# Score priority, a whole-bank norm and moved conditioning products in a two-layer decoder kernel

## The chip, the cores and the metric

The kernel runs on one core of one Trainium2 chip. The metric is the device time of one execution in microseconds (us); less is better. It is told as the median of several executions.

## What is computed

Two layers of a conditioned decoder trunk on a sequence of 256 tokens with 1024 features, all in float32. Each layer is three sublayers: a half-step SwiGLU FFN, a token mixer, and another half-step FFN. The mixer of the first layer is a gated linear recurrence (HGRN2), that of the second a causal gMLP. Every sublayer is wrapped in two RMS norms, and in a shift, a scale and a gate that come from a conditioning vector c.

```python
def sublayer(x, fn, pre_g, post_g, shift, scale, gate, res_w):
    h = rms_norm(x, pre_g) * (1.0 + scale) + shift
    return x + res_w * gate * rms_norm(fn(h), post_g)

mod = (silu(c) @ ada_w[i] + ada_b[i]).reshape(B, 9, D_MODEL)   # shift, scale, gate x 3

# recurrence, per chunk of 64 tokens and head (8 heads of 128)
o_inter = einsum('bhtk,bhkv->bhtv', qb * exp(bb), state)
decay   = exp(where(causal, bb[t] - bb[s], -inf))
scores  = einsum('bhtk,bhtsk,bhsk->bhts', qb, decay, kb)
o       = o_inter + einsum('bhts,bhsv->bhtv', scores, vb)
out     = (rms_norm(o, out_norm) * silu(g)) @ w_out            # norm per head
```

## The kernel before

**Sublayers and tiles.** The sublayers run one after the other: ffn0, the recurrence (called hg), ffn1, ffn2, the gMLP (gm), ffn3. Tokens lie in two tiles t of 128 rows; a tile of the result y is two halves h of 512 columns, each a bank of PSUM. Every matrix product is made of three matmuls on operands that are split into a high and a low part (L160 to L164 with 512 columns, L441 to L445 with 256, L400 to L420 for the first products of a sublayer, `pps`).

**Weights.** A weight block of 128x2048 comes in two halves. Each half is a 512 KB load `raw` on the SP queue (L57; four raw buffers, loads in program order), a cast to the high part on ACT (`cast`, L113 to L128), and a subtraction for the low part on DVE (`sub`, L129 to L135). `halves(n)` does n of both.

**Conditioning products.** The modulation is 144 products of 128x1024 on DVE (`ada`, L179 to L196; the product and the read-out of its sum are two rows at L192), each with a 512 KB load of its own on the SP queue and three buffers. `pace(upto, blocks, skip)` (L154) spreads them over the weight blocks of a sublayer, up to the cumulative target of the table `bgs` in `run`; the users `gate_tile` (L212, called through `G_fn`) and `pre_cols` (L197) force what is still missing when they are called.

**Boundary.** `boundary` (L297) leads from one sublayer to the next. Its instructions on ACT, DVE and PE stand in the hand-written order of the code: last products of y, squares of y (L233 to L236), mean and root, residual (L251), squares of x, the scaled row xn (L290), its transposes `npa` on PE (L264 to L277), the high part of h on ACT, and the full `hf` and the low part of h on DVE (L278 to L289). Everything else is ordered by the scheduler of the framework, by priority in program order.

**Recurrence.** `hgrn` (L627) first makes the projections `fps` and `tps` and the gates (`gate_f`, L666). `attn` (L693) then works one half of the heads (hb = 0, 1): for seven levels it scales q and k on DVE and ACT (tiles `t`), multiplies them on PE into scores (`ab`, L741, 64 columns; L701 and L761, 128 columns), merges each level's block by copy_predicated on DVE (L712), and at last multiplies the scores with v (L774, L776; called PV below). `finish` (L781) takes the norm per head (128-column squares on ACT, L787; a product from PSUM on DVE for each 128 columns, L800), transposes the result on PE (`ots`, L805) and splits it (L809, L810) for the output product y (`out_mm`, L395). `zip_steps` (L837) interleaves the generator of `attn` with fill work: projections of the second half, and for the second loop the products `outs` of the first half.

**gMLP.** `gmlp` (L912) makes the v half, calls `G_fn`, loads three columns of constants and then runs the u half in units.

## Time and profile before

| | |
|---|---|
| executions | 1199.64, 1200.78, 1204.22 us; median 1200.78 |
| the profiled execution | 1199.71 us, span 1197.9 us |
| PE busy | 1144.4 us, 96% of the span |
| DVE busy | 909.9 us, 76% |
| ACT busy | 663.3 us, 55% |
| bytes moved | 282.31 MB, 236 GB/s in the mean |
| granted clock of PE, mean | 0.982 |

The profile's lines name a line of the kernel, an engine, an operation and its tiles as out<-in. PE is TensorE, PEld its weight loads, DVE is VectorE, ACT is ScalarE, SP the queue that issues the loads. Behind a group stands the idle time of its engine just before it and what ended it. The waits view groups PE's idle time by the waiting line and by what it waited for: total, times, longest. A window's row gives each engine's busy time, then the granted clock of PE, the share of DMA and GB/s.

### The profile page before, as it was taken

The page shows a single profiled execution, that of the slowest core. Times are in us where ns is not written, and L with a number is a line of the kernel's source. Part 1 is how long each engine was busy: PE and PEld are TensorE (multiplying, and loading weights), DVE is VectorE, ACT ScalarE, POOL GpSimd, SP SyncE. Part 2 cuts the span into 40 slices and gives each one's busy share as a digit, 9 for nine tenths or more (in the row PEclk, how much of TensorE's full clock was granted, in tenths as well). Part 3 has the DMA queues.
Part 4 walks back from the last instruction along what each step waited for, and adds up shares of the span by engine and source line. Part 5 has one row for each costly group of instructions (what it writes and reads, how often), then busy time and mean ns, then how long its engine had stood idle before and what let it go on. Part 6 is the DMA issues. An engine that isn't in the chain of part 4 may idle for free.

```text
span 1197.9 us, 17119 instructions
## 1 busy us (share of the span) xinstructions
PE 1144.4 (96%) x6518; PEld 997.4 (83%) x6518; DVE 909.9 (76%) x1391; ACT 663.3 (55%) x1054; POOL 6.8 (1%) x16
## 2 busy tenths in 40 slices
PE   7999998898798899999999999999999999999997
PEld 6989997798787688888788888877798997888886
DVE  6987786779867789985589986476898777866642
ACT  6454446668547755555565555553664456645531
POOL 0000000000000000000000000000000000000000
PEclk9999999898899999999999999999999999999999
DMA  9889898296305389986279996426687764766630
GB/s 349 311 315 331 320 351 287 95 327 233 125 35 193 106 293 365 333 307 224 94 261 339 344 334 227 165 80 222 234 316 276 265 201 131 247 216 226 207 106 36
DMA packets 79764, 282.31 MB, mean 236 GB/s; under 512 B 9873, under 2 KB 10561, under 8 KB 79682
## 3 DMA queue, kind: packets, MB, share of 16 engines
q1 hardware_dynamic: 78626, 278.05, 66.0%
q0 software_dynamic: 1056, 3.17, 0.8%
q8 instruction: 51, 0.84, 0.3%
q14 instruction: 31, 0.25, 0.1%
HBM read 280.11 MB, written 1.07 MB: 235 GB/s over the span
## 4 chain that ended last, share of the span: by engine, by line
PE 83%; DVE 8%; DMA 4%; ACT 4%; issue 1%; SPq 0%; DVEq 0%; ACTq 0%
PE ups L437 17%; PE ups L438 9%; PE y L162 8%; PE y L163 8%; PE y L164 8%; PE pps L412 7%; PE ups L557 4%; PE ups L445 4%; PE ups L443 4%; PE ups L444 4%; DVE w L132 2%; PE ab L741 2%; DMA raw<-in_wffn 2%; ACT w L122 1%; PE vps L1003 1%
## 5 line engine op out<-in xcount | busy, mean ns | idle before, releaser
L132 DVE TENSOR_TENSOR w<-raw,w 128x1024 fp32r<-128x1024 f32 x376 | 453.8, 1223 | 113.5 <-ACT w L122 105.5
L122 ACT CAST w<-raw 128x1024 fp32r<-128x1024 f32 x376 | 387.1, 1050 | 167.7 <-DMA raw<-in_wffn 66.0
L437 PE MATMUL ups<-h,w 128*128 128x512 f32 x864 | 302.0, 393 | 0.0
L438 PE MATMUL ups<-h,w 128*128 128x256 f32 x864 | 242.0, 280 | 0.0
L437 PEld LDWEIGHTS ups<-h,w 128*128 128x128 f32 x864 | 161.7, 187 | 36.4
L192 DVE CUSTOM_DVE_ANT_0 ada<-ada,cond 128x1024 f32<-128x1024 f32 x144 | 173.6, 1221 | 21.7 <-DMA ada<-in_ada 21.7
L162 PE MATMUL y<-w,t 128*128 128x512 f32 x448 | 179.7, 402 | 0.0
L163 PE MATMUL y<-w,t 128*128 128x512 f32 x448 | 178.2, 398 | 0.3 <-DVE w L132 0.3
L164 PE MATMUL y<-w,t 128*128 128x512 f32 x448 | 177.7, 397 | 0.0
L438 PEld LDWEIGHTS ups<-h,w 128*128 128x128 f32 x864 | 163.3, 189 | 1.0
L445 PE MATMUL ups<-h,w 128*128 128x256 f32 x416 | 117.9, 283 | 2.1 <-DVE rs_sd L89 1.2
L443 PE MATMUL ups<-h,w 128*128 128x256 f32 x416 | 118.3, 284 | 0.0
L444 PE MATMUL ups<-h,w 128*128 128x256 f32 x416 | 117.7, 283 | 0.0
L412 PE MATMUL pps<-w,h 128*128 128x512 f32 x480 | 115.1, 396 | 0.2 <-DVE h L287 0.2
L412 PEld LDWEIGHTS pps<-w,h 128*128 128x128 f32 x480 | 89.9, 190 | 19.2 <-DVE h L287 0.6
L164 PEld LDWEIGHTS y<-w,t 128*128 128x128 f32 x448 | 84.6, 189 | 20.3
L162 PEld LDWEIGHTS y<-w,t 128*128 128x128 f32 x448 | 84.7, 189 | 18.9
L163 PEld LDWEIGHTS y<-w,t 128*128 128x128 f32 x448 | 84.7, 189 | 18.9 <-DVE w L132 1.4
L445 PEld LDWEIGHTS ups<-h,w 128*128 128x128 f32 x416 | 79.7, 191 | 2.5 <-DVE w L132 2.5
L443 PEld LDWEIGHTS ups<-h,w 128*128 128x128 f32 x416 | 79.7, 192 | 1.0 <-issue 0.2
L444 PEld LDWEIGHTS ups<-h,w 128*128 128x128 f32 x416 | 79.7, 192 | 0.8 <-issue 0.2
L80 ACT ACTIVATE t<-t 128x256 f32<-128x256 f32 (+2 forms) x70 | 36.6, 524 | 50.4 <-DVE t L490 41.7
(196 smaller groups left out, 1327.1 us busy)
## 6 DMA issues: line engine op xcount, KB each, us to landing
raw<-in_wffn SPq DMA_DIRECT2D x264, 512.0 KB, 5.5
ada<-in_ada SPq DMA_DIRECT2D x144, 512.0 KB, 6.7
raw<-in_wgmu SPq DMA_DIRECT2D x48, 512.0 KB, 5.0
raw<-in_whg SPq DMA_DIRECT2D x40, 512.0 KB, 5.2
raw<-in_wgmv SPq DMA_DIRECT2D x24, 512.0 KB, 5.0
G<-gflat POOLq DMA_DIRECT2D x6, 512.0 KB, 5.1
t<-in_gbin SPq DMA_DIRECT2D x6, 256.0 KB, 5.6
x<-in_x SPq DMA_DIRECT2D x2, 512.0 KB, 4.3
```

Of the source, the lines that this page charges most:

```text
L122: self.after(self.nc.scalar.copy(hi[:, sl], raw), self.hold[0])
L132: self.after(self.nc.vector.tensor_sub(lo[:, sl], raw, hi[:, sl]), self.hold[1])
L162: self.paced(mm(ps, l[0], r[0], start=start, stop=False))
L163: mm(ps, l[0], r[1], start=False, stop=False)
L164: mm(ps, l[1], r[0], start=False, stop=stop)
L192: self.after(nc.vector.tensor_tensor_reduce(t, t, self.cond, 1.0, 0.0, ALU.mult, ALU.add, self.mod[i // 24][:, i % 24:i % 24 + 1]), self.h ...
L412: lambda g=g, i=i, j=j, kc=kc, w=w: mm(res[g][t], h2[:, i, t, kc, :], w, start=kc + i + j == 0, stop=i == 1 and kc == KC - 1)))
L437: self.paced(mm(ps, u[0], self.h2[:, :, :, kc, :], start=kc == 0, stop=False))
L438: self.last = mm(ps[:, 1, :], u[1], self.h2[:, 0, :, kc, :], start=False, stop=kc == KC - 1)
L443: self.paced(mm(o, u[0], h[0], start=start, stop=False))
L444: mm(o, u[0], h[1], start=False, stop=False)
L445: self.last = mm(o, u[1], h[0], start=False, stop=stop)
```

## The change

- *Scores:* the steps of `attn` are wrapped in a raised scheduler priority (offset 400).
- *Norm:* `finish` is split into `stats`, `turn` and `split`. The squares are one ACT instruction for a whole bank into SBUF, with a sum on DVE; the gate product is one DVE instruction for a bank, and the scale by r is made on SBUF. For the second half of the heads all of this stands in a hand-written order, with 5 of the 16 output products ahead, 1 between the two groups of transposes, and the rest behind.
- *Boundary:* the mean of the squares of x is taken after both halves; the second half's `hf` is made on ACT; its low part comes behind the residual of the second tile; 35 instead of 30 products of the next sublayer stand ahead of the second transposes; how many casts stand where is a parameter.
- *Conditioning:* cumulative targets 40 after ffn0 (was 46) and 120 after ffn2 (was 118); in the recurrence they are spread over 14 blocks (was 9).
- *gMLP:* `G_fn` moves into the u loop (u = 8), and the three constants are loaded in ffn0.

```diff
@@ residual, h_low
-                if h == 0:
-                    self.half_mean(st)
+        if st is not None:
+            self.half_mean(st)
...
+    def h_full(self, h, pa, cols, scalar=False):
...
+            if scalar:
+                nc.scalar.activation(hf[:, ks], pa[:, ks], AF.Identity, bias=sh[:, kc:kc + 1], scale=A[:, kc:kc + 1])
+            else:
+                nc.vector.tensor_scalar(hf[:, ks], pa[:, ks], A[:, kc:kc + 1], sh[:, kc:kc + 1],
+                                        op0=ALU.mult, op1=ALU.add)
+        return hf
@@ boundary
+    def boundary(self, y, G, mm, cols, table, plan=(4, 2, 0, 0)):
...
-        self.halves(4)
+        self.halves(plan[0])
...
-        self.halves(2)
+        self.halves(plan[1])
...
+        for _ in range(plan[2]):
+            self.cast()
         self.residual(0, yg, r, sx)
+        for _ in range(plan[2]):
+            self.sub()
...
-        self.h_low(0, 0, pa0, cols)
-        self.h_low(0, 1, pa1, cols)
-        w = [[self.ready.pop(0) for _ in range(2)] for _ in range(2)]
-        self.res, go = self.proj(w)
+        self.h_low(0, 0, self.h_full(0, pa0, cols))
         sq(1, 1, sy1)
         gated(1, 1, yg1)
         r = self.inv_rms(sy1)
-        self.cast()
+        for _ in range(plan[3]):
+            self.cast()
+        hf = self.h_full(1, pa1, cols, scalar=True)
         self.residual(1, yg1, r, sx1)
-        self.sub()
+        for _ in range(plan[3]):
+            self.sub()
+        self.h_low(0, 1, hf)
+        w = [[self.ready.pop(0) for _ in range(2)] for _ in range(2)]
+        self.res, go = self.proj(w)
...
-        do(p0[0:30])
+        do(p0[0:35])
...
+        self.halves(1)
         self.table(table)
@@ hgrn
-        self.pace(bg, 9)
+        self.pace(bg, 14)
...
+        def attn(hb, bank, res):
+            gen = attn_steps(hb, bank, res)
+            while True:
+                with tc.high_priority(offset=400):
+                    if next(gen, gen) is gen:
+                        return
+                yield
...
+        def stats(hb, ops, sqrt):
...
+            for u in range(2):
+                sqs.append(self.t2().rearrange("p (i v) -> p i v", i=4))
+                nc.scalar.activation(sqs[u], ops[u].rearrange("p t h v -> p (t h) v"), AF.Square)
...
+                nc.vector.tensor_mul(og[:, 512 * u:512 * u + 512].rearrange("p (t c) -> p t c", t=NT),
+                                     ops[u].rearrange("p t h v -> p t (h v)"), gg[:, :, c0:c0 + 2 * P])
...
+                nc.vector.reduce_sum(ss[:, 4 * u:4 * u + 4], sqs[u], axis=mybir.AxisListType.X)
...
+        def turn(hb, u, og, r):
+            on = og[:, 512 * u:512 * u + 512].rearrange("p (i v) -> p i v", i=4)
+            for i in range(4):
+                nc.vector.tensor_scalar(on[:, i, :], on[:, i, :], r[:, 4 * u + i:4 * u + i + 1], None, op0=ALU.mult)
+            ps = self.acc.tile([P, 512], F32, tag="acc", name="ots")
...
-        finish(1, ops[1], True)
+        self.ahead = 0
+        fill = products(1)
...
+        self.open()
+        self.gate = state["ops"]
+        for op in fill[:5]:
+            op()
+        og, r = stats(1, ops[1], True)
+        ps = [turn(1, 0, og, r)]
+        fill[5]()
+        ps.append(turn(1, 1, og, r))
+        self.sub()
+        for op in fill[6:]:
+            op()
@@ gmlp
-        G = G_fn()
...
+            if u == 8:
+                G = G_fn()
@@ run
-        bgs = {"ffn0": 46, "hg": 64, "ffn1": 92, "ffn2": 118, "gm": 138, "ffn3": 144}
+        bgs = {"ffn0": 40, "hg": 64, "ffn1": 92, "ffn2": 120, "gm": 138, "ffn3": 144}
...
+                    self.boundary(y, G, mm, st["cols"], tables[subs[s + 1][0]], (2, 1, 1, 1) if s == 1 else (4, 2, 0, 0))
```

Lines behind L258 have other numbers in the changed kernel: scores are L758 (before L741), merges L729 (L712), `ots` L845 (L805), and the scale by r is L841.

On ACT at the end of ffn0, before; `t` is the last unit's activation there, `junka` takes the squares of y and of x:

```order
L80 ACTIVATE t_2008<-ups 128x512
L122 CAST w<-raw 128x1024 x3
L167 CAST t_2009<-t_2008 128x512
L74 ACT_TABLE_LOAD
L122 CAST w<-raw 128x1024 x9
L235 ACTIVATE junka,s_2091<-y_784 128x512
L122 CAST w<-raw 128x1024 x2
L235 ACTIVATE junka,s_2091<-y_785 128x512
```

The same place in the changed kernel:

```order
L80 ACTIVATE t_1996<-ups 128x512
L122 CAST w<-raw 128x1024 x4
L167 CAST t_1997<-t_1996 128x512
L74 ACT_TABLE_LOAD
L122 CAST w<-raw 128x1024 x6
L235 ACTIVATE junka,s_2079<-y_790 128x512
L122 CAST w<-raw 128x1024 x2
L235 ACTIVATE junka,s_2079<-y_791 128x512
```

Nine casts stood between the table load and the first square, and six stand there now; the other three come earlier.

On PE in the second score loop, before, where the first half's result is transposed (`ots`), with scores `ab` of two levels around it:

```order
L164 MATMUL tps<-w,h_2198 128x512
L741 MATMUL ab<-t_3441 128x64 x8
L805 MATMUL ots<-ident,t_3495 128x128 x4
L805 MATMUL ots<-ident,t_3509 128x128 x4
L741 MATMUL ab<-t_3521 128x64 x8
L162 MATMUL y_3536<-w 128x512
```

The same place in the changed kernel:

```order
L164 MATMUL tps<-w,h_2186 128x512
L845 MATMUL ots<-ident,t_3452 128x128 x5
L758 MATMUL ab<-t_3506 128x64 x8
L758 MATMUL ab<-t_3553 128x64 x8
L845 MATMUL ots<-ident,t_3452 128x128 x3
L162 MATMUL y_3521<-w 128x512
```

The transposes now stand ahead of the scores of two levels, and the level that came just ahead of them before (t_3441, now t_3435) is done earlier among the `tps` products.

On DVE in the second score loop, before, up to the first products with r (L800):

```order
L735 TENSOR_TENSOR t_3413<-t_3413,w 128x32x16
L788 TENSOR_SCALAR ss_3456<-ss_3456 128x8
L88 TENSOR_SCALAR rs_sh<-ss_3456 128x8
L91 TENSOR_SCALAR rs_hv<-ss_3456 128x8
L89 TENSOR_SCALAR rs_sd<-rs_sh 128x8
L98 TENSOR_TENSOR rs_q<-rs_sd 128x8
L735 TENSOR_TENSOR t_3441<-t_3441,w 128x64x8
L712 COPY_PREDICATED t_3290<-lmask,ab 128x16x32
```

The same loop in the changed kernel, between the merge of a level (L729) and the first sum of squares (L823):

```order
L729 COPY_PREDICATED t_3275<-lmask,ab 128x32x16
L132 TENSOR_TENSOR w<-raw,w 128x1024
L192 ISA ada,mod_108<-ada,cond 128x1024
L192 ISA mod_108 128x1
L192 ISA ada,mod_108<-ada,cond 128x1024
L192 ISA mod_108 128x1
L132 TENSOR_TENSOR w<-raw,w 128x1024 x2
L192 ISA ada,mod_108<-ada,cond 128x1024
L192 ISA mod_108 128x1
L823 TENSOR_REDUCE ss_3450<-t_3453 128x4
L819 TENSOR_TENSOR t_3452<-ab,w 128x512
```

Before, no conditioning product stood between the first scores of this loop and its `ots`; now eight stand there, with subs of weights between them.

More of the change, by code (lines that the diff above doesn't have):

```diff
@@ L295, in scaled, with open @@
             self.nc.scalar.activation(xn[:, hs], self.x[t][:, hs], AF.Copy, scale=r)
-    def boundary(self, y, G, mm, cols, table):
-        nc = self.nc
+    def open(self):
         E = mybir.EngineType
@@ L779, in attn @@
             yield
-        def finish(hb, ops, sqrt=False):
+        def attn(hb, bank, res):
[6 more added lines that the diff above has]
+        def stats(hb, ops, sqrt):
             ss = self.tiny.tile([P, 8], F32, tag="ss8", name="ss8")
-            o4 = [o.rearrange("p t h v -> p (t h) v") for o in ops]
+            r = self.tiny.tile([P, 8], F32, tag="r8", name="r8")
+            og, sqs = self.t4(), []
@@ L784, in finish, with gated @@
             for u in range(2):
-                for i in range(4):
-                    junk = self.scr.tile([P, 512], BF16, tag="junka", name="junka")
-                    nc.scalar.activation(junk[:, 0:P], o4[u][:, i, :], AF.Square, accum_out=ss[:, 4 * u + i:4 * u + i + 1])
+                sqs.append(self.t2().rearrange("p (i v) -> p i v", i=4))
+                nc.scalar.activation(sqs[u], ops[u].rearrange("p t h v -> p (t h) v"), AF.Square)
+            def gated(u):
+                c0 = 2 * (2 * hb + u) * P
+                nc.vector.tensor_mul(og[:, 512 * u:512 * u + 512].rearrange("p (t c) -> p t c", t=NT),
+                                     ops[u].rearrange("p t h v -> p t (h v)"), gg[:, :, c0:c0 + 2 * P])
@@ L788, in finish @@
+            for u in range(2):
+                nc.vector.reduce_sum(ss[:, 4 * u:4 * u + 4], sqs[u], axis=mybir.AxisListType.X)
+                if u == 0:
+                    gated(0)
             nc.vector.tensor_scalar(ss, ss, 1.0 / P, EPS, op0=ALU.mult, op1=ALU.add)
-            r = self.tiny.tile([P, 8], F32, tag="r8", name="r8")
             if sqrt:
                 self.tact(ss, ss, AF.Sqrt)
+                self.cast()
+                gated(1)
                 nc.vector.reciprocal(r, ss)
@@ L793, in finish @@
             else:
+                gated(1)
                 self.rsqrt(r, ss)
[L795 to L811 removed]
@@ new lines, in stats @@
+            return og, r
+        def turn(hb, u, og, r):
[3 more added lines that the diff above has]
+            ps = self.acc.tile([P, 512], F32, tag="acc", name="ots")
+            for i in range(4):
+                c0 = (i % 2) * S + (i // 2) * P
+                nc.tensor.transpose(ps[:, c0:c0 + P], on[:, i, :], self.ident)
+            return ps
@@ L813, in hgrn, with split @@
+        def split(hb, u, ps):
+            pair = 2 * hb + u
+            if not oall:
+                oall.extend([self.wtile() for _ in range(2)])
+            oT = [o[:, 512 * pair:512 * pair + 512] for o in oall]
+            nc.scalar.activation(oT[0], ps, AF.Copy, scale=self.onorm)
+            nc.vector.scalar_tensor_tensor(oT[1], ps, self.onorm, oT[0], op0=ALU.mult, op1=ALU.subtract)
+            oTs.append([o.rearrange("p (h s) -> p h s", h=2) for o in oT])
         ybank = {"i": 0}
@@ L907, in hgrn @@
         wos.append(nb())
+        self.open()
[8 more added lines that the diff above has]
+        for op in fill[6:]:
+            op()
+        for u in range(2):
+            split(1, u, ps[u])
         nxt(y, G, self.out_last(y, oTs[2:], wos))
@@ L1083, in late_consts @@
         self.onorm = self._load("onorm", [P, 1])
+        self.gm_cols = [self._load(n, [P, 24]) for n in ("gbinu", "glng", "glnb")]
     def first_h(self, kc):
@@ L1127, in nxt @@
                 else:
-                    self.boundary(y, G, mm, st["cols"], tables[subs[s + 1][0]])
+                    if s != 1:
+                        self.open()
+                    self.boundary(y, G, mm, st["cols"], tables[subs[s + 1][0]], (2, 1, 1, 1) if s == 1 else (4, 2, 0, 0))
                     self.hT = self.h2[:, 0], self.h2[:, 1]
```

67 lines of the change are left out of this document (24 added, 43 removed).

## Prediction

> **What bounds the kernel now.** I read the page first, then PE's waits, then the granted clock, then single stretches. The page says whose time it is:
>
> ```profile
> PE 1144.4 (96%) x6518; PEld 997.4 (83%) x6518; DVE 909.9 (76%) x1391; ACT 663.3 (55%) x1054; POOL 6.8 (1%) x16
> ```
>
> PE works for all but 53.5 of the span's 1197.9 us, and the change removes no matrix product. So it can pay only in idle time of PE and in time at a lowered clock. The waits of PE, grouped (total, times, longest), name the idle time that the edits aim at:
>
> ```profile
> PE npa L271 <- DVE be L242: 9.7, 2, 8.1
> PE npa L271 <- DVE xn L293: 7.5, 4, 2.4
> PE ab L741 <- DVE t L735: 6.6, 1, 6.6
> PE ab L741 <- ACT L L679: 5.1, 1, 5.1
> PE ots L805 <- DVE t L800: 5.0, 1, 5.0
> ```
>
> The windows cut where the granted clock changes show the second cost. After its name each row has the length, PE busy, PEld, DVE, ACT, POOL, clock, DMA share, GB/s:
>
> ```profile
> 208.79:219.03 10.24, 5.52 (x17) 4.63 (x18) 5.97 (x16) 5.95 (x16) 0.00 (x0) 0.50 0.40 142
> 287.29:297.53 10.24, 8.37 (x39) 8.40 (x40) 9.91 (x19) 7.63 (x20) 0.00 (x0) 0.50 0.72 252
> 311.19:321.43 10.24, 6.76 (x24) 6.12 (x25) 8.82 (x16) 5.22 (x7) 0.00 (x0) 0.50 0.28 100
> 382.87:386.28 3.41, 3.41 (x11) 2.37 (x11) 3.15 (x9) 1.91 (x3) 0.00 (x0) 0.50 0.46 156
> 410.17:413.59 3.42, 3.42 (x12) 2.72 (x11) 3.21 (x6) 2.25 (x7) 0.00 (x0) 0.50 0.63 165
> 840.25:843.67 3.42, 3.42 (x10) 2.66 (x9) 3.42 (x4) 1.67 (x4) 0.52 (x1) 0.50 0.71 242
> ```
>
> At clock 0.50, u us of busy PE do the work of u/2, so these stretches cost 2.8, 4.2, 3.4, 1.7, 1.7 and 1.7. Losses by place: **A**, ffn0 to recurrence, 8.1 + 2.8 = 10.9. **B**, the score stalls of the recurrence, 5.1 + 6.6 + 4.2 + 3.4 = 19.3. **C**, the last `ots` transposes, 5.0 + 1.7 = 6.7. **D**, recurrence to ffn1, (9.7 - 8.1) + 2.4 + 1.7 = 5.7. **E**, the three later boundaries, 7.5 - 2.4 = 5.1. **F**, start of the gMLP's u half, 3.7 (rows there).
>
> **The change part by part.** *A.* PE, then ACT, then the chain of waits:
>
> ```profile
> 213.51 1.11 PE L271 MATMUL npa<-ident,xn 128*128 128x128 f32 x4 [8.09 <-DVE be L242]
> ```
>
> ```profile
> 202.04 0.59 ACT L235 ACTIVATE junka<-y 128x512 bf16<-128x512 f32 x1
> 207.17 0.59 ACT L235 ACTIVATE junka<-y 128x512 bf16<-128x512 f32 x1
> ```
>
> ```profile
> 183.35 6.53 DMA raw<-in_wffn
> 192.42 5.84 DMA raw<-in_whg
> 200.63 5.57 DMA raw<-in_whg
> ```
>
> ```profile
> 160.00:180.00 20.00, 20.00 (x146) 18.91 (x146) 15.74 (x20) 7.89 (x11) 0.56 (x1) 1.00 0.98 345
> ```
>
> Row squares stand behind casts on ACT, casts behind weights that land late, in a stage whose DMA is full (0.98). Six fewer conditioning loads (46 to 40) take 6 x 512 KB, at 345 GB/s 9.1 us, out of that queue. In ACT's order three of nine casts move ahead of the table load before the first square. Taking the mean after both halves saves about 0.8 more. Needed: 8.1. I take a gap of 0.4 without half clock: gain 10.5. Least gain 3.3 (mean 0.8, two subs fewer at 1.22), if casts or the four raw buffers, not DMA, set the pace; most 10.9. Should the squares become early, the next late thing is the residual chain; ffn1 to ffn2 has the same chain and no first gap.
>
> *Recurrence, B.* Prices:
>
> ```profile
> L132 DVE TENSOR_TENSOR w<-raw,w 128x1024 fp32r<-128x1024 f32 x38 | 45.6, 1224 | 9.3 <-ACT w L122 9.2
> L192 DVE CUSTOM_DVE_ANT_0 ada<-ada,cond 128x1024 f32<-128x1024 f32 x18 | 21.5, 1223 | 0.8 <-DMA ada<-in_ada 0.8
> L712 DVE COPY_PREDICATED t<-lmask,ab 128x512 f32<-128x512 int32 x14 | 12.6, 899 | 13.1 <-PE ab L741 12.9
> L735 DVE TENSOR_TENSOR t<-t,w 128x512 f32<-128x512 f32 x14 | 9.7, 691 | 0.9 <-ACT t L80 0.9
> L800 DVE SCALAR_TENSOR_TENSOR t<-ab,r,w 128x128 f32<-128x128 f32 x16 | 4.4, 345 | 0.1
> ```
>
> ```profile
> 289.17 1.09 PE L741 MATMUL ab<-t 128*128 128x64 f32 x4 [5.09 <-ACT L L679]
> ```
>
> ```profile
> 202.17 1.23 DVE L132 TENSOR_TENSOR w<-raw,w 128x1024 fp32r<-128x1024 f32 x1 [0.21 <-ACT w L122]
> 203.31 0.15 DVE L242 TENSOR_SCALAR be<-s 128x1 f32<-128x1 f32 x1
> ```
>
> ```profile
> 204.79 0.40 PE L163 MATMUL y<-w,t 128*128 128x512 f32 x1
> 205.02 0.39 PE L164 MATMUL y<-w,t 128*128 128x512 f32 x1
> ```
>
> With priority the first score loop becomes one burst on DVE: 19 operations of 512 columns (0.691), 7 merges (0.899), 2 of half width (0.35 each by halving), one conditioning product and one sub (1.3, 1.2), 2 others (0.7). That is 24, less 0.09 of overlap for each of 32 (the sub at 202.17 lasts 1.23, its successor starts after 1.14): about 21. Begun near 288, where the stall that ends at 289.17 lies, it ends at 309, and PE does not wait 6.6 in between. B's 19.3 is thus won here.
>
> But the moved work falls on the second loop. Between the end of the first and the norm's first scale, DVE's new order has 8 subs (9.8), 10 conditioning products (13.1 with their read-out), 17 operations of 512 (11.7), 4 merges (3.6), 14 gate steps of 256 or 512 columns (8.0, by 0.3 to 0.7 each), 2 products of the output gate and 2 sums (2.8), 2 adds of the identity (1.4) and some 20 tiny ones (3.5): 54, less 85 x 0.09, so 46.4. DVE reaches the scale at 309 + 46.4 = 355.4. PE meanwhile has 73 products of 512 at 0.233 (204.79 to 205.02) = 17.0, 32 of 64 columns and 25 of 128 (4.3 and 7, by 0.14 to 0.28 each): 28 to 30, and waits about 2.8 for the scores of level 64 (half of the 5.1 at the first level before). So it is at the five `ots` transposes, which now stand ahead of the scores of levels 4 and 2, at 337 to 342; I take 341. PE stalls there 14.5 (13.5 to 18.5), 17.3 with level 64, then 3.4 of clock as after the 6.6 before: 20.7 lost. **B: 19.3 - 20.7 = -1.4.** DVE in the whole stage, before:
>
> ```profile
> 232.30:397.50 165.20, 146.54 (x954) 134.39 (x952) 133.41 (x225) 105.90 (x193) 1.08 (x2) 0.93 0.53 185
> 334.50:397.50 63.00, 56.16 (x334) 48.71 (x334) 48.49 (x91) 40.14 (x87) 0.69 (x2) 0.97 0.37 126
> ```
>
> Six products add 7.9 and the norm about 3 to its 133.4, some 144 of the stage's 165, while PE without losses needs 146.5 less the 9.3 of half clock, 137: DVE becomes the tighter engine there. At best, with its work spread, the stage loses nothing in the second loop: +19.3 for B.
>
> *C.* The norm was 8 squares and 8 products of 128 columns from PSUM (0.345) for a half; now two whole-bank squares (0.59, as the square at 202.04), two sums, two gate products and 8 scales. The sum has no row: between 0.15 (202.17's successor) and 0.899; I take 0.69, as an add of the same width. The scale of 128 columns from SBUF: 0.15 to 0.345; I take 0.25. Chain to the first four transposes: 2 x 0.59 + 2 x 0.69 + 0.69 + 0.15 + 0.3 + 0.15 + 4 x 0.25 = 4.9 with handovers 5.5; the 15 products put ahead cover 3.5. Gap 2.0 instead of 5.0. Gaps of 1.6 to 2.0 brought no half clock, one of 2.4 did (the stretch at 410.17), so I count part of 1.7: C gains 3.0 (0 to 6.7). The Trainium skill, "TensorE: Matmul & The Clock Gate", section "Why this matters for your kernels", puts the gap that halves the clock at over about 3 us; by it this term would be 3.7 and not 3.0, but the 2.4 us gap here shows that less is enough. The same skill, "VectorE: DVE Perf Modes", section "Rules for kernel authors", calls a reduce the slowest operation and advises against it on a hot path, which speaks against the two sums; at the merge's 0.9, the slowest row of that width, each adds 0.2, and the term would be 2.6. No run here shows a reduce of this form.
>
> *D.* One cast and two subs (1.05 + 1.22 + 1.22) now stand ahead of the second half's low part of h, which the 20th product of the next stage needs just in time elsewhere: a wait of about 3.5 and 1.7 of clock, for 5.7 before: +0.4 (-2 to +5.7). Recurrence in all: -1.4 + 3.0 + 0.4 = **2** (-5 to +24).
>
> *E.* PE waits at the boundary ffn1 to ffn2, and DVE there:
>
> ```profile
> 598.80 0.66 PE L271 MATMUL npa<-ident,xn 128*128 128x128 f32 x4 [1.57 <-DVE xn L293]
> ```
>
> ```profile
> 591.65 1.37 DVE L284 TENSOR_SCALAR hf<-npa,A,shift 128x128 f32<-128x128 f32 x4
> 593.06 0.69 DVE L287 TENSOR_TENSOR h<-hf,h 128x512 fp32r<-128x512 f32 x1
> 596.00 0.15 DVE L242 TENSOR_SCALAR be<-s 128x1 f32<-128x1 f32 x1 [0.79 <-ACT junka L235]
> ```
>
> The `hf` and sub from 591.65 leave the chain (2.0), the mean's wait at 596.00 goes (0.8): 2.85 earlier, and five more products ahead of the transposes (5 x 0.233 = 1.2) cover: no gap at three places. The sub now comes behind the residual, due about when it is needed: I charge 0.3. **4.8** (2.5 to 5.1).
>
> *F.* DVE, then PE:
>
> ```profile
> 834.61 1.23 DVE L192 CUSTOM_DVE_ANT_0 ada<-ada,cond 128x1024 f32<-128x1024 f32 x1 [4.81 <-DMA ada<-in_ada]
> ```
>
> ```profile
> 837.79 0.27 PE L219 MATMUL gps<-ident,gate 128*8 128x128 f32 x1 [1.15 <-DVE w L924]
> 838.93 0.50 PE L163 MATMUL pps<-w,h 128*128 128x512 f32 x1 [0.86 <-DVE w L132]
> ```
>
> The gate needs 120 products and only 118 were done; DVE stands 4.8 for the load of the last two with `w` behind it. Now 120 are done in ffn2, where two more (2.6 us of DVE) hide behind a PE that is never idle, and the gate is built later: 1.15 + 0.86 + 1.7 = **3.7** (1 to 4.5).
>
> *Three small loads* go into ffn0's start, where DMA is full: -0.5 (-1.5 to 0; most: the raw wait of one weight).
>
> **Sum.** 10.5 + 2 + 4.8 + 3.7 - 0.5 = 20.5. The profiled execution took 1199.71 us (1.1 under the median of 1200.78), so 1179.2, against the median 1180.
>
> **The rivals.** *1, the second loop does not stall:* DVE runs ahead of my count (13.1 us of idle before merges, in the L712 row, could take the products), `ots` finds its tile ready, the recurrence gains 2 + 17: 1163. For it: 165 - 144 = 21 us of slack in the stage. Against: the products stand in DVE's order behind the first burst. *2, casts or buffers set the pace at A:* gain 3.3 there instead of 10.5: 1187. For it: casts end each link of the chain in turn; against: full DMA. *3, slower:* in the second loop DVE waits for each conditioning load with three buffers, and everything up to `ots` waits behind it. The longest such wait in the trace is 6.4:
>
> ```profile
> DVE ada L192 <- DMA ada<-in_ada: 21.7, 9, 6.4
> ```
>
> Five such add 32 at `ots`: 1212. It decides once that stall passes 14.5 + 20.5 = 35, and is over the bound below at 41. Against: the DMA share there, 0.37. *4, little comes:* the recurrence at -2, A 3.3, E 2.5, F 1, the small loads -1: 3.8, so 1197.
>
> **How the numbers follow.** Mine 0.54, rival 1 0.22, rival 2 0.13, rival 3 0.05, rival 4 0.06. The range takes my case, rival 2 and part of rival 1: 1161 to 1193. A measurement here can tell 0.5%, 6 us, from no change: faster (under 1194.8) 0.88, same 0.07, slower 0.05.
>
> **What would show it.** PE's wait before the first transposes of h for the recurrence under 1 (A); no wait before scores in the first loop; a wait of some 14 before `ots` in the second loop, with half clock behind it (B; none is rival 1, over 35 rival 3); about 2 before the last `ots` (C); a wait of `pps` for the low part of h at recurrence to ffn1 (D); no wait of `npa` at the three later boundaries (E); none of DVE for a conditioning load in the gMLP (F). A time outside 1161 to 1193 would refute the sum; no stall at `ots` would refute B's count.

## The result, and the profile after

The changed kernel takes 1190.51 us in the median of four executions (1187.75 to 1192.97), the kernel before 1202.49 beside it. The ratio is 0.9911, 95% interval [0.9888, 0.9933]. The profiled executions stand 1187.75 against 1199.71: 12.0 us less, where the prediction's sum said 20.5. The time lies inside the range, and the gain is 59% of what the sum had.

The page, then PE's waits of the changed kernel (total, times, longest):

```profile
span 1186.0 us, 17085 instructions
...
PE 1138.3 (96%) x6518; PEld 992.1 (84%) x6518; DVE 906.2 (76%) x1379; ACT 665.9 (56%) x1046; POOL 6.8 (1%) x16
```

```profile
PE ots L845 <- DVE t L841: 18.1, 2, 15.6
PE vps L1059 <- DVE t L1066: 4.4, 4, 2.1
...
PE pps L429 <- DVE h L293: 3.1, 1, 3.1
...
PE tps L163 <- DVE w L132: 2.3, 1, 2.3
...
PE npa L271 <- DVE be L242: 2.2, 2, 1.9
...
PE fps L462 <- DVE w L132: 0.8, 1, 0.8
PE ab L718 <- DVE t L719: 0.7, 1, 0.7
```

The two waits of scores (6.6 and 5.1) are gone, and so is every wait of `npa` for xn (7.5). In their place stands one wait of 15.6 us at the first `ots`. The wait of `vps` in the gMLP is new; the prediction had nothing there.

The windows of the changed kernel at the lowered clock; the first row is the entry of the recurrence, the second stands behind the wait of `tps`, and the last two are the parts of one stretch before and after PE resumes at `ots`:

```profile
206.97:210.38 3.41, 3.41 (x12) 2.73 (x11) 1.71 (x6) 2.54 (x7) 0.00 (x0) 0.50 0.41 163
...
312.78:319.61 6.83, 5.71 (x13) 4.47 (x14) 6.81 (x10) 4.94 (x12) 0.55 (x1) 0.50 0.52 182
...
340.09:353.50 13.41, 0.00 (x0) 0.03 (x1) 13.24 (x38) 2.11 (x2) 0.00 (x0) 0.50 0.55 193
353.50:363.98 10.48, 10.48 (x45) 9.99 (x46) 6.38 (x13) 5.40 (x7) 0.00 (x0) 0.50 0.66 228
```

By u/2 they cost 1.7, 2.9 and 5.2. While PE stands still from 340.09 to 353.50, DVE is busy for 13.24 of 13.41 us: it is late, not idle.

The losses of PE by place, idle time and half clock, from the waits and the clock of both traces; gain is before less after:

| place | before | after | gain | forecast |
|---|---|---|---|---|
| start of ffn0 (idle) | 8.7 | 9.4 | -0.7 | -0.5 |
| A, entry of the recurrence | 8.1 + 2.8 | 1.9 + 1.7 | 7.3 | 10.5 |
| recurrence, with C and the exit's first wait | 18.7 + 9.3 | 22.5 + 8.1 | -2.7 | 1.6, and a part of D |
| exit, second part | 2.6 + 1.7 | 3.1 + 0 | 1.3 | rest of D's 0.4 |
| E, three later boundaries | 5.1 | 0 | 5.1 | 4.8 |
| F, gMLP | 4.1 + 1.7 | 4.4 + 0 | 1.4 | 3.7 |
| end | 6.3 | 6.4 | -0.1 | 0 |

Together 11.6 of the 12.0 us. Half clock at the start of ffn0 is left out of the first row: in both kernels the first products there take 0.42 us each instead of 0.28, for a stretch that cost about 0.8 us less in the changed kernel's profile.

### The profile page after: what moved, and what is told of

It is laid out like the page before. It is cut to its first block, busy times and chain, and to the rows that moved or that the text cites. A ratio compares the mean times of both kernels' runs of the same rounds, so it can differ in the third digit from the quotient of the medians.

```text
span 1186.0 us, 17085 instructions
## 1 busy us (share of the span) xinstructions
PE 1138.3 (96%) x6518; PEld 992.1 (84%) x6518; DVE 906.2 (76%) x1379; ACT 665.9 (56%) x1046; POOL 6.8 (1%) x16
## 4 chain that ended last, share of the span: by engine, by line
PE 78%; DVE 8%; DMA 8%; ACT 4%; issue 2%; SPq 0%; DVEq 0%; ACTq 0%
PE ups L454 16%; PE ups L455 8%; PE y L163 8%; PE y L164 8%; PE y L162 8%; PE pps L429 7%; PE ups L574 4%; DVE w L132 3%; PE ups L460 3%; PE ups L462 3%; PE ups L461 3%; PE ab L758 2%; DMA ada<-in_ada 2%; DMA raw<-in_wffn 2%; DMA raw<-in_wgmu 2%
## 5 line engine op out<-in xcount | busy, mean ns | idle before, releaser
L163 PEld LDWEIGHTS y<-w,t 128*128 128x128 f32 x448 | 84.5, 189 | 19.3 <-DVE w L132 1.5
```

Of the source, the lines that this page charges most:

```text
L163: mm(ps, l[0], r[1], start=False, stop=False)
```

## The experiments

All ratios are to the kernel before, measured beside it. The recurrence in the texts below is the time from the second transposes of its entry to the first of its exit: 171.6 us before, 174.3 after. In kernels with the new boundary it begins five products later, which makes it 1.2 us shorter by definition.

| kernel | ratio, 95% interval | recurrence | wait at entry | longest at ots |
|---|---|---|---|---|
| before | 1 | 171.6 | 8.1 | 5.0 |
| changed | 0.9911 [0.9888, 0.9933] | 174.3 | 1.9 | 15.6 |
| pace9 | 0.9965 [0.9948, 0.9982] | 177.9 | 2.4 | 5.5 |
| pace5 | 1.0202 [1.0183, 1.0220] | 210.1 | 2.8 | 5.5 |
| bg46 | 0.9946 [0.9931, 0.9961] | 170.9 | 7.3 | 10.6 |
| noprio | 0.9848 [0.9834, 0.9863] | 166.8 | 3.6 | 8.8 |
| b_bg | 0.9963 [0.9945, 0.9980] | 173.5 | 2.3 | 5.7 |
| b_prio | 0.9961 [0.9946, 0.9976] | 165.0 | 8.1 | 3.2 |
| b_bound | 0.9865 [0.9844, 0.9886] | 164.8 | 6.0 | 5.4 |
| np_pace11 | 0.9878 [0.9850, 0.9905] | 171.6 | 3.0 | 4.7 |
| s46p9 | 0.9896 [0.9869, 0.9923] | 167.1 | 7.4 | 7.5 |
| n46p9 | 0.9838 [0.9820, 0.9856] | 161.6 | 7.6 | 1.2 |
| np_plan32 | 0.9813 [0.9789, 0.9837] | 166.8 | 2.2 | 8.9 |
| bound_gm | 0.9836 [0.9818, 0.9855] | 163.9 | 7.1 | 5.3 |
| bound_gm_prio | 0.9848 [0.9819, 0.9877] | 165.2 | 7.6 | 3.7 |
| best46 | 0.9837 [0.9814, 0.9860] | 162.9 | 8.0 | 1.2 |
| best42 | 0.9821 [0.9793, 0.9848] | 167.9 | 3.0 | 5.1 |
| best43 | 0.9873 [0.9842, 0.9904] | 168.8 | 4.8 | 0.4 |
| prio_norm | 0.9918 [0.9893, 0.9943] | 171.8 | 4.1 | 0.7 |
| np_pn | 0.9860 [0.9840, 0.9880] | 169.4 | 2.6 | 3.5 |

### What makes the wait at ots: pace9, pace5, bg46, noprio

pace9, and pace5 with 5 in the same place:

```diff
-        self.pace(bg, 14)
+        self.pace(bg, 9)
```

> The changed kernel with the recurrence's 24 conditioning products spread over 9 weight blocks instead of 14. DVE's order then has 6 of them, not 10, between the first score loop and the scale ahead of the first ots. Theory P (place): the wait of PE at ots, 15.6 us in the changed kernel, is made of what stands ahead of it on DVE, about 1.3 us for each product; the wait becomes 10 to 11, and with less half clock the time falls by 5 to 9 us, a ratio to the kernel before of about 0.985. Theory T (total): DVE's work in the whole recurrence is the limit, so what leaves this place delays the gates and the first scores by as much; the wait shrinks, other waits grow, and the ratio stays at 0.991.

PE's waits of pace9:

```profile
PE ots L845 <- DVE t L841: 8.0, 2, 5.5
...
PE tps L162 <- DVE w L707: 2.9, 1, 2.9
...
PE fps L462 <- DVE w L132: 2.7, 1, 2.7
```

The wait at `ots` falls by 10 us, more than the four products' 5.2, and the kernel is slower than the changed one, 0.9965 with an interval that lies above the other's. Projections now wait (fps, tps) and the recurrence takes 3.6 us more. Place is what makes the one wait, and not what makes the loss: theory T.

> The same with 5 blocks: none of the products stands between the first score loop and the first ots, all are done during the first projections. Theory P: the wait at ots falls below 4 us and its half clock goes, 15 to 20 us less than the changed kernel, ratio about 0.976. Theory T: PE waits as long in the first part of the recurrence, for gates and scores, ratio about 0.99.

PE's waits of pace5:

```profile
PE fps L460 <- ACT w L122: 17.7, 4, 8.7
PE ots L845 <- DVE t L841: 7.9, 2, 5.5
```

With all products in the first projections PE waits there, 17.7 us at one line, with half clock at each of the three long waits (2.3 to 8.7). 1.02: slower than before, and further from theory P than theory T had it.

bg46:

```diff
-        bgs = {"ffn0": 40, "hg": 64, "ffn1": 92, "ffn2": 120, "gm": 138, "ffn3": 144}
+        bgs = {"ffn0": 46, "hg": 64, "ffn1": 92, "ffn2": 120, "gm": 138, "ffn3": 144}
```

> The changed kernel with 46 conditioning products in the first sublayer again, so 18 in the recurrence, 5 of them ahead of the first ots. Both theories: the wait at ots falls by 6 to 8 us. At the boundary ffn0 to recurrence: if the full DMA made the gap of the kernel before (theory D), it is back at 6 to 8 us (1.9 in the changed kernel) and the ratio is 0.990 to 0.993; if the order of casts and the later mean removed it (theory C), it stays near 2 and the ratio is about 0.984.

PE's waits of bg46:

```profile
PE ots L845 <- DVE t L841: 13.1, 2, 10.6
PE npa L271 <- DVE be L242: 7.7, 2, 7.3
```

The entry's wait is back at 7.3: the six loads made it, and the later mean, which is in this kernel, did not remove it. (What the mean is worth can't be read off: with 46 products and the new boundary the wait is 6.0 to 8.0 us in the table.) Theory D holds against the mean, but not against the casts: with 46 products the scheduler puts nine casts ahead of the first square again, so that full DMA and the place of three casts come and go together and were not told apart. The wait at `ots` falls by 5.0, a little less than expected, and the recurrence by 3.4. So six products are worth 5.4 of wait and 1.0 of clock at the entry (2.7 against 1.7) and cost 3.4 in the recurrence. Another 3.1 of the 6.3 us by which bg46's profile is the longer one is half clock behind the wait of 3.07 at the exit, which the changed kernel has too, without half clock (last section).

noprio (`if True:` in place of the line with `tc.high_priority`):

```diff
-                with tc.high_priority(offset=400):
+                if True:
```

> The changed kernel without the raised priority of the score steps. Theory P: the wait at ots falls to 3 or less, since 6 products and only 2 subs stand between, but the waits before scores, 5.1 and 6.6 in the kernel before, come back with two stretches of half clock: as fast as the changed kernel within 4 us, ratio 0.988 to 0.995. Rival: the priority as such made the wait at ots and gained nothing, ratio below 0.98.

PE's waits of noprio in the recurrence:

```profile
PE ots L845 <- DVE t L841: 10.2, 2, 8.8
...
PE ab L758 <- ACT t L80: 2.7, 1, 2.7
```

Faster than the changed kernel, and the intervals lie apart: 0.9848 against 0.9911. Theory P had the score waits of the kernel before come back, and they did not: 2.9 is left of 11.7. Nor did the wait at `ots` fall to 3, as the same theory had it: 6 products and 2 subs leave 8.8. The rival's ratio, below 0.98, was not reached either. The priority is not needed for the score waits to go.

### What removed the score waits: b_bg, b_prio, b_bound, best43

b_bg, in the kernel before:

```diff
-        self.pace(bg, 9)
+        self.pace(bg, 14)
...
-        bgs = {"ffn0": 46, "hg": 64, "ffn1": 92, "ffn2": 118, "gm": 138, "ffn3": 144}
+        bgs = {"ffn0": 40, "hg": 64, "ffn1": 92, "ffn2": 118, "gm": 138, "ffn3": 144}
```

> The kernel before with two numbers of the change alone: target 40 instead of 46 after ffn0, and the recurrence's products over 14 blocks instead of 9. Theory V (the prediction's: the priority of the scores removed the score stalls): the waits of ab for DVE and ACT, 11.7 us in the kernel before, stay within 3 us of that; only the boundary ffn0 to recurrence gains, ratio about 0.993. Theory W (moving products out of the first projections removed them): those waits fall below 4 us, with their two stretches of half clock, and the ratio is about 0.982.

PE's waits of b_bg:

```profile
PE ots L805 <- DVE t L800: 11.5, 2, 5.7
...
PE ab L741 <- ACT t L80: 2.0, 1, 2.0
PE ab L741 <- DVE t L735: 1.9, 1, 1.9
```

The score waits fall to 3.9, as theory W has it, but the ratio is 0.9963 and not 0.982: two waits of 5.7 at `ots` take their place, and PE's idle time in the recurrence is 17.8 us beside 18.7 before. Its gain is the entry's alone.

b_prio puts the priority's wrapper alone into the kernel before:

```diff
-        def attn(hb, bank, res):
+        def attn_steps(hb, bank, res):
...
+        def attn(hb, bank, res):
+            gen = attn_steps(hb, bank, res)
+            while True:
+                with tc.high_priority(offset=400):
+                    if next(gen, gen) is gen:
+                        return
+                yield
```

> The kernel before with the raised priority of the score steps alone. Theory V: the waits of ab fall below 4 us and the ratio is below 0.99. Theory W: the waits only move, to the first ots or to the projections (fps, tps) whose casts and subs are pushed back, and the ratio is 1.00 or above.

PE's waits of b_prio:

```profile
PE ots L814 <- DVE t L809: 4.7, 2, 3.2
...
PE ab L741 <- ACT t L80: 1.7, 1, 1.7
```

The score waits go here too, and the recurrence gains 6.6. Neither theory had that together with a ratio of 0.9961: of the 6.6 the medians show 4.7, and the gMLP takes 2.4 us longer than in the kernel before.

b_bound puts the new boundary alone (mean, `h_full`, order, 35 products) into the kernel before, with (4, 2, 0, 0) everywhere. Of its edit only the call is shown; the rest is that of the change:

```diff
-                    self.boundary(y, G, mm, st["cols"], tables[subs[s + 1][0]])
+                    self.open()
+                    self.boundary(y, G, mm, st["cols"], tables[subs[s + 1][0]], (4, 2, 0, 0))
```

> The kernel before with the new boundary alone (mean after both halves, hf of the second half on ACT, its low part later, 35 products ahead), with its casts and subs placed as in the other boundaries everywhere. The prediction: no wait of npa at the three later boundaries (5.1 us less), 0.8 less at the boundary out of ffn0, whose gap stays at 7 to 8; ratio 0.994 to 0.996. Rival: the full DMA gives the time back in the next sublayer's start, ratio 0.998 to 1.00.

PE's waits of b_bound:

```profile
PE npa L271 <- DVE xn L299: 6.0, 1, 6.0
PE ots L822 <- DVE t L817: 5.4, 1, 5.4
...
PE fps L460 <- ACT w L122: 3.1, 1, 3.1
...
PE ab L758 <- ACT t L80: 2.0, 1, 2.0
```

The one part does more than the whole change: 0.9865 against 0.9911. The later boundaries are free of waits as forecast, the entry's is 6.0 instead of 8.1 (forecast 0.8 less), and the score waits are down to 2.0 although no line of the recurrence was touched. So three edits, each alone, take away 8 to 10 of the same 11.7 us. That is not all gain: in b_bound 3.7 us of waits of `fps` for weights stand just ahead of the first scores instead, and PE's idle time in the whole recurrence, 18.7 us before, is 17.8 in b_bg, 12.7 in b_prio and 12.0 in b_bound. What the three have in common is that the scheduler lays out the recurrence anew. The first score loop on PE, in runs of one tile:

```
before      tps 12, ab 8, tps 12, ab  8, tps 12, ab 8, tps 12, ab 28
b_bound     tps 12, ab 8, tps 12, ab 16, tps 13, ab 8, tps 12, ab  8
noprio      tps 12, ab 8, tps 12, ab 16, tps 15, ab 8, tps 12, ab  8
best43      tps 12, ab 8, tps 12, ab  8, tps 12, ab 8, tps 12, ab 28
```

best43 is a kernel with the new boundary, norm and gMLP part and without priority that happens to get the layout of the kernel before:

```diff
-        self.pace(bg, 14)
+        self.pace(bg, 11)
...
-        bgs = {"ffn0": 40, "hg": 64, "ffn1": 92, "ffn2": 120, "gm": 138, "ffn3": 144}
+        bgs = {"ffn0": 43, "hg": 64, "ffn1": 92, "ffn2": 120, "gm": 138, "ffn3": 144}
```

(beside noprio's line and np_plan32's below).

> As best42 with 43 products and 11 blocks. The scheduler then lays out PE's first score loop as in the kernel before (12 tps, 8 ab, 12 tps, 28 ab) and not as in all other runs without priority (16 ab after 12 tps). Theory O: the long waits before scores, 5.1 and 6.6 us there, come with that layout and are back here, though boundary, norm and targets are new; the recurrence takes 170 us or more, ratio 0.985 to 0.990. Rival (the new boundary or the fewer early products removed them): waits of ab below 4 us, ratio about 0.981.

PE's waits of best43 in the recurrence:

```profile
PE ab L758 <- DVE t L752: 7.3, 2, 6.6
PE ab L758 <- ACT L L696: 7.0, 1, 7.0
```

The two waits are back at the same places, 6.6 and 7.0 for 6.6 and 5.1, with a stretch of 10.2 us at half clock at each as before. The recurrence is at 168.8, a little under the expected 170.

DVE's order shows what makes the later wait. Before, the scale that these scores need (L735, at 313.83) stands behind two subs and the six gate steps of the second half; in best42 (below; 42 products and 12 blocks) the scale of the same level (L752) stands ahead of them:

```profile
308.81 2.36 DVE L132 TENSOR_TENSOR w<-raw,w 128x1024 fp32r<-128x1024 f32 x2
...
313.83 0.69 DVE L735 TENSOR_TENSOR t<-t,w 128x512 f32<-128x512 f32 x1
```

```profile
299.35 0.68 DVE L752 TENSOR_TENSOR t<-t,w 128x512 f32<-128x512 f32 x1
...
301.17 2.35 DVE L132 TENSOR_TENSOR w<-raw,w 128x1024 fp32r<-128x1024 f32 x2
```

best43 has the order of the kernel before, b_bg and b_bound that of best42. So the wait of 6.6 goes with the layout, and edits that have nothing to do with the scores change the layout. For the earlier wait this is not shown: best42 still waits 4.6 us at the first scores.

### Why the priority costs: s46p9, n46p9, bound_gm_prio, prio_norm

s46p9 has bg46's line and pace9's; n46p9 has noprio's as well.

> The changed kernel, priority and new norm included, with the old targets in its first half: 46 products in the first sublayer, 18 in the recurrence over 9 blocks. Theory I (the priority pays or costs by what is left for behind the first score burst): only 3 products stand there, the wait at ots is below 4 us, the recurrence (second transposes of its entry to first of its exit) takes 163 to 167 us against 174.3 in the changed kernel and 165.0 with priority alone in the kernel before; the gap at its entry is back at 7 us; ratio 0.986 to 0.990. Rival (the new norm and its place make the priority costly): recurrence 170 us or more, ratio 0.993 or above.

> The same without the priority. Theory I: the score burst does not run ahead, nothing is left behind it either; recurrence 163 to 167 us, the same as with the priority within 3 us, ratio 0.985 to 0.990. Rival (priority is needed where the products come early): waits of scores of 5 us and more come back and the recurrence takes 170 us or more.

PE's waits of s46p9, then of n46p9:

```profile
PE ots L845 <- DVE t L841: 10.0, 2, 7.5
```

```profile
PE ots L845 <- DVE t L841: 2.3, 2, 1.2
```

At the old targets too the priority costs: recurrence 167.1 with it, 161.6 without. That is better than theory I for n46p9, and s46p9 has about the expected length (163 to 167), but not the expected wait below 4 at `ots`.

bound_gm (below) with b_prio's wrapper:

> bound_gm (new boundary, gMLP part, old norm, old targets; 0.9836) with the raised priority of the score steps. Theory O (each edit makes the scheduler lay out the recurrence anew; the long score waits belonged to the layout of the kernel before, the boundary's layout no longer has them, and the priority then only delays the projections' weights and the norm): slower than bound_gm by 3 to 8 us, ratio 0.986 to 0.990. Theory N (the priority costs only beside the new norm): as fast as bound_gm or faster, ratio 0.984 or below.

0.9848 against 0.9836, with intervals that overlap, and 1.2 us in the recurrence: with the old norm the priority costs next to nothing on top of the new boundary. Theory O was wrong on this cost. Beside the new norm and its hand-written order it is 5.5 us at 18 products and 7.5 at 24. Each of these kernels is one layout, so that a layout by chance is not ruled out as the cause.

prio_norm gives the first half's norm the same priority in the changed kernel:

```diff
-            og, r = stats(0, ops[0], False)
-            for u in range(2):
-                split(0, u, turn(0, u, og, r))
+            with tc.high_priority(offset=400):
+                og, r = stats(0, ops[0], False)
+                ps = [turn(0, u, og, r) for u in range(2)]
+            for u in range(2):
+                split(0, u, ps[u])
```

> The changed kernel with the first half's norm (its squares, sums, gate products, root, scale and transposes) at the same raised priority as the scores. Theory L (the new norm waits because everything without priority, 10 products and 8 subs, is mixed in ahead of it, while the scores are pulled ahead): 7 products stand ahead of the scale instead of 10, the three between the steps of the root are gone, the wait at ots falls from 15.6 to about 11 and the ratio from 0.9911 to about 0.987. Rival (DVE has that much to do before ots whatever its order): the wait stays at 14 or more, ratio 0.990 to 0.993.

PE's waits of prio_norm in the recurrence:

```profile
PE y L162 <- ACT w L853: 11.6, 1, 11.6
PE tps L163 <- DVE w L132: 6.8, 2, 4.5
...
PE ots L845 <- DVE t L841: 1.0, 2, 0.7
```

The wait at `ots` is gone, as theory L would have it, and it stands at the last output product instead, 11.6 us, with 4.5 more at a weight. The ratio is the changed kernel's, 0.9918. Neither theory had the wait at `y`, but the rival's point holds: PE's idle time in the recurrence is 21.5 us, 22.5 in the changed kernel. With the scores raised it is paid at one place or another.

DVE's share in the recurrence says part of why. The same window, cut at each kernel's own boundaries, before and in the changed kernel, and without priority at 24 and at 18 products (noprio, n46p9):

```profile
225.93:397.48 171.55, 152.89 (x985) 139.71 (x984) 138.63 (x235) 111.90 (x205) 1.08 (x2) 0.93 0.51 178
```

```profile
219.03:393.28 174.25, 151.77 (x980) 137.35 (x978) 147.81 (x254) 106.91 (x176) 1.08 (x2) 0.91 0.54 187
```

```profile
221.28:388.06 166.78, 151.81 (x980) 138.75 (x979) 146.33 (x254) 107.11 (x176) 1.08 (x2) 0.93 0.58 196
```

```profile
227.32:388.95 161.63, 150.46 (x980) 137.07 (x979) 140.94 (x242) 106.94 (x176) 1.07 (x2) 0.96 0.54 183
```

PE's work without half clock is 143.3 to 143.9 us in all four. DVE's is 138.6 before and 147.8 after: it has become the longer one. But the amount is not all: noprio has 146.3 us of it and takes 7.5 us less than the changed kernel. Its order leaves 6 products and 2 subs between the first score loop and the first `ots`, where the changed kernel has 10 and 8.

### Parts and versions: bound_gm, np_plan32, np_pace11, best46, best42, np_pn

bound_gm is b_bound with the gMLP part (gate at u = 8, target 120 after ffn2, constants early):

```diff
-        G = G_fn()
...
+            if u == 8:
+                G = G_fn()
...
-        bgs = {"ffn0": 46, "hg": 64, "ffn1": 92, "ffn2": 118, "gm": 138, "ffn3": 144}
+        bgs = {"ffn0": 46, "hg": 64, "ffn1": 92, "ffn2": 120, "gm": 138, "ffn3": 144}
```

> The kernel before with the new boundary (as in b_bound, 0.9865) and the gMLP part: the gate built at u = 8, 120 products after the third FFN, the three constants loaded early. The prediction: 3.7 us less than b_bound, ratio about 0.983. Rival (the loads come as late as before, and the wait returns at vps, as the 4.4 us in the changed kernel): within 2 us of b_bound, ratio 0.985 to 0.988.

PE's wait of bound_gm in the u half:

```profile
PE vps L1017 <- DVE t L1024: 1.9, 1, 1.9
```

PE's loss in the gMLP falls from 6.5 (4.8 and 1.7 of clock) to 2.3, and the ratio from 0.9865 to 0.9836; the intervals overlap, so the 4 us are the profile's. They are the 3.7 forecast. In the changed kernel the part leaves 4.4 at `vps`, and in other kernels 1.1 to 4.5.

np_plan32, beside noprio's line:

```diff
-                    self.boundary(y, G, mm, st["cols"], tables[subs[s + 1][0]], (2, 1, 1, 1) if s == 1 else (4, 2, 0, 0))
+                    self.boundary(y, G, mm, st["cols"], tables[subs[s + 1][0]], (3, 2, 0, 0) if s == 1 else (4, 2, 0, 0))
```

> The changed kernel without priority and with the recurrence's exit boundary as the others have it (3 and 2 halves before the first two row squares, no cast and sub around the residuals, instead of 2, 1, 1, 1). The prediction's reading of that wait (one cast and two subs ahead of the low part of h): the wait of pps for h, 3.1 us, falls to 1 or less, 2 to 4 us less, ratio about 0.982. Rival: the two more halves ahead of the squares delay these, npa waits 2 to 3 us instead, ratio 0.985.

PE's wait of np_plan32 at the exit:

```profile
PE pps L429 <- DVE h L293: 1.0, 1, 1.0
```

The wait falls from 3.1 to 1.0, as the prediction's reading of it has it (one cast and two subs ahead of the low part of h), while the exit's first wait of `npa` grows from 0.4 to 1.4, a part of what the rival had. 0.9813 is the best ratio of all, and its interval lies clear of the changed kernel's. Against noprio it isn't shown to be faster: the intervals overlap, and the profiled executions take 1179.83 and 1179.35 us.

np_pace11, noprio with 11 blocks:

```diff
-        self.pace(bg, 14)
+        self.pace(bg, 11)
```

> The changed kernel without the priority and with the products over 11 blocks instead of 14, so that 3 instead of 6 stand between the first score loop and the first ots. Theory P: the wait at ots, 8.8 us without priority, falls to about 5, and the ratio is about 0.981 (0.9848 without priority). Theory T: what leaves there comes back as waits of the projections or scores, ratio 0.984 to 0.988.

Wait at `ots` 4.7 instead of 8.8, recurrence 171.6 instead of 166.8, ratio 0.9878: theory T again, at the upper end of its range; the interval overlaps noprio's. As in pace9, products that come earlier make projections wait (fps 3.0 and 1.9) and cost more than they free.

best46 is n46p9 with np_plan32's line; best42 is np_plan32 with 42 for 40 after ffn0 and 12 blocks for 14.

> The changed kernel without priority, with the old targets 46 and 9 blocks in its first half, and with the recurrence's exit as in np_plan32. From n46p9 (0.9838), whose wait of pps was 3.1 us: 2 us less, ratio about 0.982; the gap at the recurrence's entry stays at 7 to 8.

> As np_plan32 (0.9813), with 42 products in the first sublayer and 12 blocks in the recurrence, between the two targets. If the entry gap and the recurrence's waits trade evenly, product for product (7.3 to 1.9 us for six at the entry, 2 to 5 us in the recurrence), no target is better than another by more than 2 us: ratio 0.980 to 0.983.

0.9837 and 0.9821 beside 0.9813 with 40 products: the three cannot be told apart, so the targets trade about evenly, as the second text says. best46 is not measurably better than n46p9 although its wait at the exit is 1.0.

np_pn is np_plan32 with prio_norm's lines.

> np_plan32 (0.9813: the changed kernel without the priority of the scores, exit boundary as elsewhere) with the raised priority for the first half's norm alone. Four products and 4 subs, not 6 and 2, stand between the first score loop and the scale, and the last two merges ahead of it are behind it. Theory L: the wait at ots falls from 8.9 to 5 or less, recurrence 163 to 165 us, ratio about 0.979. Rival: the scores behind it come late instead, ratio 0.981 to 0.984.

Priority for the norm alone: the wait at `ots` falls from 8.9 to 3.5, scores wait 4.4 and 2.7, the recurrence takes 169.4, ratio 0.9860. The rival, and a little worse than it.

## Why the prediction was off, point by point

**The total.** Most places of loss were read rightly, and the sum was too high by 8.5 us of 20.5. Three terms failed: A by 3.2, the recurrence by 3.3 in all, F by 2.3. The small loads (-0.7 for -0.5) and E (5.1 for 4.8) came as worked out.

**A** (10.5, measured 7.3). That the six products made the gap is shown by bg46 (7.3 with them); whether by the full DMA itself or by the casts that then stand in another order stays open. The step that failed is the gap of 0.4 without half clock. 1.9 is left, with 1.7 of half clock behind it, and in the other kernels with 40 products the wait is 2.2 to 4.1. The chain of waits of the changed kernel shows two subs between the two row squares and the second gate product:

```profile
200.06 2.35 DVE w L132 x2
202.41 0.60 DVE yg L319
```

The prediction named the residual chain as the next late thing and charged it 0.4; the two subs of 1.2 us ahead of the gate product, which the boundary's own order puts there, were not in that chain.

**B, the ots wait.** "DVE reaches the scale at 355.4", "PE stalls there 14.5". Measured: the wait is 15.6 us; the rows ahead of the scale and its first one:

```profile
346.51 1.22 DVE L192 CUSTOM_DVE_ANT_0 ada<-ada,cond 128x1024 f32<-128x1024 f32 x1
...
347.80 1.22 DVE L192 CUSTOM_DVE_ANT_0 ada<-ada,cond 128x1024 f32<-128x1024 f32 x1
...
349.02 1.22 DVE L192 CUSTOM_DVE_ANT_0 ada<-ada,cond 128x1024 f32<-128x1024 f32 x1
...
351.32 1.23 DVE L192 CUSTOM_DVE_ANT_0 ada<-ada,cond 128x1024 f32<-128x1024 f32 x1
...
353.07 1.07 DVE L841 TENSOR_SCALAR t<-t,r 128x128 f32<-128x128 f32 x5
```

Four products stand between the steps of the root of 8 numbers, as the order had them. The whole runs 8.0 us earlier than the kernel before by then (the first `fps` product starts at 233.80, before at 241.82), so the scale at 353.1 is 361.1 in the prediction's frame, nearly 6 later than worked out; PE comes later by about as much, and the wait is the same.

**B, the rest.** The half clock was charged 3.4 "as after the 6.6 before" and cost 8.1: 5.2 behind `ots`, where it lasts 10.48 us after PE resumes, and 2.9 behind a wait of 2.3. That wait (`tps` for a weight) stands in place of the 2.8 charged for level 64; waits of 0.8 and 0.7 were not foreseen. B's loss was 27.5 where 20.7 was worked out: 19.4 of waits and 8.1.

**B, the cause.** "With priority the first score loop becomes one burst" and "B's 19.3 is thus won here": the burst is real, and as the cause it fell. noprio, b_bg and b_bound lose the score waits without it, and best43 has them again with the old layout. The wait of 6.6 belonged to one layout of the scheduler; of the one of 5.1 a part stays or moves to `fps` in some of the new ones, and its cause stays open. The prediction charged the new order with what it saw of it, and took the old order's waits for a property of the kernel.

**Six products in the recurrence.** "DVE becomes the tighter engine there" was right, as the windows with 24 products show (147.8 and 146.3 beside 143.7 and 143.3 of PE's work). The rival in which the second loop doesn't stall fell. The two runs that took the wait away from `ots` and kept the priority, pace9 and prio_norm, were no faster. Both amount and order count: six products fewer shorten the recurrence by 3.4 us (bg46), and by 5.2 without priority (n46p9 against noprio, with 9 blocks instead of 14), and the order without priority by 7.5 with all 24 in it.

**C** (3.0, measured 4.1). The last `ots` waits 2.55 for the 2.0 worked out, and no half clock follows. The 3.0 was the gap's gain with all 1.7 of half clock kept, not a part of it; without half clock the prediction's own terms give 4.7, and not the 3.7 that it names. **D** (0.4, measured 2.5). The wait of `pps` is 3.07 for 3.5, again with no half clock, and the exit's first wait fell from 1.56 to 0.36. These two gave back 3.2 of what B lost.

**The sums' price** was a guess between bounds; its row, and that of the scale:

```profile
L841 DVE TENSOR_SCALAR t<-t,r 128x128 f32<-128x128 f32 x16 | 3.3, 281 | 0.1
...
L823 DVE TENSOR_REDUCE ss<-t 128x4 f32<-128x512 f32 x4 | 2.7, 681 | 0.0
```

0.68 for a sum, as taken (0.69). The objection of the Trainium skill ("VectorE: DVE Perf Modes", "Rules for kernel authors") that a reduce is the slowest operation does not hold at this size: it takes what an add of the same width does (0.69).

**F** (3.7, measured 1.4). All four waits of the kernel before at that place are gone, 4.1 and 1.7 of clock, more than forecast. But waits of `vps` came in the u half, 4.4 us. DVE there, before the longest of them (2.1):

```profile
899.63 1.23 DVE L192 CUSTOM_DVE_ANT_0 ada<-ada,cond 128x1024 f32<-128x1024 f32 x1 [3.04 <-DMA ada<-in_ada]
900.78 0.08 DVE L192 DVE_READ_ACCUMULATOR2_ANT mod<- 128x1 f32 x1
900.78 0.48 DVE L1066 SCALAR_TENSOR_TENSOR t<-vps,glng,bc 128x256 f32<-128x256 f32 x1
```

A product that waits 3.04 us for its load stands ahead of the operation that frees the buffer of `vps`. The prediction followed the two products only as far as the gate, and not the 18 that remain into the u half. The other kernels with the part wait 1.1 to 4.5 us there against the 5.8 lost before; what sets that was not tried.

## What to carry to other kernels

A wait in a kernel whose order a scheduler makes may belong to that one layout: before an edit is credited with removing it, make an unrelated edit alone, since here three different ones each took away 8 to 10 of the same 11.7 us. Look at the stage's whole idle time too, and not at the one wait: in b_bg it hardly fell. Where a second engine has become the longer one in a stage (DVE 148 us beside 144 of PE's work), moving or prioritizing single pieces moved the wait, from `ots` to `fps` or to `y`; what shortened the stage was less work in it, and an order that doesn't pull one part ahead of the rest. Run each part of a bundle alone: here the boundary was worth 13.5 permille and the whole with the priority 8.9.

## What the runs showed of the hardware

How long a wait must be for the clock to halve is no fixed number. Stretches at 0.50 are multiples of 3.41 us, and their start does not follow the wait's length: 1.86 us at the entry of the changed kernel was followed by 3.41 us, 2.30 (with 0.68 shortly before) by 6.83, while 2.55 and 3.07 were followed by none. The same wait of 3.06 to 3.07 us at the exit cost 3.1, 2.9, 1.7, 1.6 and 1.5 us of half clock more in bg46, pace9, np_pace11, pace5 and s46p9, and none in the changed kernel, noprio, n46p9 and prio_norm. The Trainium skill, "TensorE: Matmul & The Clock Gate", section "Why this matters for your kernels", gives over about 3 us as the limit; a wait of 1.86 was enough here. After the long wait of 15.58 the clock stayed halved for 10.48 us of work, after 5.09 and 6.64 in the kernel before for 8.37 and 6.76.

What decides it can be worked out from the traces. All stretches of a trace begin on one grid of 3.41 us. Cut along their grids, the 20 traces have 6403 windows at full clock between 20 and 1150 us. In 75 PE was busy for less than 0.43 of the window, and half clock followed each time; in 6241 it was busy for 0.68 or more, and half clock never followed; of the 87 between, it followed 14. So what counts is how a wait falls on the grid: the one at the exit left PE busy for 0.15 to 0.42 of one window in the five kernels that paid, and for 0.43 or more of each in the four that did not. Two profiles can differ there by 1.5 to 3.1 us without any difference in the kernels' order.
